# Front, retention, attention plan, MLP entry and the second MLP product's loads of a hybrid decoder block rearranged

## The chip, the cores and the metric

The kernel runs on one core of one Trainium2 chip. The metric is the device time of one execution in microseconds (us). A core has a matrix engine (TensorE, PE in the rows; its weight loads are PEld), VectorE (DVE), ScalarE (ACT), GpSimd (POOL) and SyncE (SP), which here only issues transfers (DMA).

## The reference, cut to what matters

One decoder block over 1024 tokens of width 1024, in fp32. Eight heads of causal differential attention and four heads of chunked retention run on one projection of the normed input; sigmoid gates merge them; then come a squared-ReLU MLP and a gate by a second embedding p.

```python
h = rms_norm(x, g_mix)
qa, ka, va, qr, kr, vr, gr, gate_a, gate_r = split(h @ w_in)
attn = softmax(c=0) - lam * softmax(c=1), causal ALiBi, then @ va      # 8 heads, 128 query rows at a time
ret  = chunkwise retention of qr, kr, vr (4 heads, chunks of 128), normed per head, times silu(gr)
mix  = sigmoid(gate_a) * (attn @ w_branch_diff) + sigmoid(gate_r) * (ret @ w_branch_ret)
x = x + mix @ w_out
x = x + square(relu(rms_norm(x, g_mlp) @ w_ff1)) @ w_ff2
x = x + gate(rms_norm(x, g_ple) @ w_ple_gate) * (p @ w_ple)
out = rms_norm(x, g_final)
```

## The kernel before

**Arithmetic.** Each fp32 operand is split into a high and a low part (`split`: a cast on ScalarE, L122, and a subtraction on VectorE, L123), and each product is three passes: high by high, high by low, low by high. The large products are Strassen-like: 2 x 2 blocks, with sums of blocks made on VectorE before they are split. A `product` (L303) and a `product_n` (L311) are 12 matmuls of 128x512; an `n_steps` (L200 to L202) or `t_steps` (L186 to L188) is 24 of them.

**Stages, in the order of the code.** (1) The front: rows of x are normed and turned (`norm_row`, L395), the products that make va and vr run (`va_first`, `v_first`, `v_rest`), and between them `fill` takes pieces of p @ w_ple from a queue (`pe_steps`, L443 and L454). A result bank of `v_first` is emptied by `v_spill`, a split on ScalarE and VectorE into the tile s2 ("s" in the rows). (2) 16 units of the in-projection, each with its block sums from `unit_prep`. (3) Retention, a head at a time: `ret_scores`, then `ret_chain` over eight chunks (L793), which ends in a norm (L801), then `ret_turn` (L810, evacuated at L813), with pieces of the gates' projection from the queue between (a queue step is six matmuls of 128x512). (4) Attention: 64 tiles of 128 queries, `scores` of the next tile (L860, its softmax on VectorE at L862 to L873, with exp on ScalarE), transposes of the last (`turn`, L887) and its product with v (`weigh`, L902), with gate pieces between. `PLAN` says how many queue steps a tile runs, `LAST` how many follow the 64th tile. (5) The branch products (`diff_half`), w_out in two sweeps over the eight row blocks of 128, half of the columns each; in the second sweep each block is normed (L1094, L1096), turned (L1104) and, from block 4 on, turned into five sums of blocks that the MLP wants (L1126 to L1132). (6) The first MLP product, 16 units (L303), the second (L1232), and the gate by p, whose product p @ w_ple is read back from `pe_d`.

Every engine runs its instructions in order, and that order is the order of the code, which the tile scheduler changes in places by the buffers. Tiles named S0 to S11, T0 to T7, Ga, Gb, s2, o, sq, raw, wh and wl are places in SBUF that one user after another takes. Banks of PSUM are named in

```python
BANKS = {"mm": 2, "qk": 3, "sm": 2, "po": 1}
```

so a third product that asks for "mm" waits until the first one's bank is emptied.

Of the kernel before, what the change touches and what calls it, by code (L numbers as in the profile page):

```python
# [36 lines left out]
PLAN = ((2, 2, 2, 2, 2, 2, 2, 2),) * HA  # L37
LAST = 16
# [24 lines left out]
def block_kernel(ctx: ExitStack, tc: tile.TileContext, t):  # L63
# [32 lines left out]
    pe_d = spill("pe_d", ST, D)  # L96
# [336 lines left out]
    def pe_steps():  # L433
        wph, wpl = [slot(s, F32R).rearrange("p (k n) -> p k n", k=2) for s in ("S10", "S11")]
        pT = [slot(s, F32R).rearrange("p (k s) -> p k s", k=2) for s in ("S6", "S9")]
        w = wp.rearrange("p (k n) -> p k n", k=2)
        for k in range(2):
            split(w[:, k, :], wph[:, k, :], wpl[:, k, :])
        for half in range(2):
            for k in range(2):  # L440
                pt = bank("sm")
                for j in range(4):
                    nc.tensor.transpose(out=pt[:, j * P:(j + 1) * P],  # L443
                                        in_=pn[:, half * 4 + j, k * P:(k + 1) * P], identity=ident)
                split(pt, pT[0][:, k, hs(half)], pT[1][:, k, hs(half)])
        yield
        for st in range(ST):
            ss_ = slice(st * P, (st + 1) * P)
            for n0 in (0, HALF):
                pe = bank("qk")  # L450
                mm = [(a[:, k, ss_], w[:, k, n0:n0 + HALF]) for k in range(2)
                      for a, w in ((pT[0], wph), (pT[0], wpl), (pT[1], wph))]
                for i, (l, r) in enumerate(mm):
                    nc.tensor.matmul(out=pe, lhsT=l, rhs=r, start=(i == 0), stop=(i == len(mm) - 1))  # L454
                o = slot("Ga", F32, (P, HALF), bufs=2)
                nc.scalar.copy(out=o, in_=pe)
# [893 lines left out]
```

## Time and profile before

| | us |
|---|---|
| median of three runs | 1982.68 (1981.89 to 1985.82) |
| the profiled execution | 1982.06 |
| its span, first to last instruction | 1980.3 |
| TensorE, 8976 matmuls, busy | 1906.2 |
| VectorE busy | 1307.5 |
| ScalarE busy | 875.9 |
| GpSimd busy | 96.4 |

Busy time of TensorE counts the overlap of pipelined matmuls, so a wait shows in the list of waits and in the idle time before a row, not in the share. The time of a run is the span and about 1.8 us around it.

### The profile page before, as it was taken

Reading aid. Unit: us, or ns where it says so; the run is one execution under the profiler, and the core shown is the slowest. Engines: PE = TensorE matmul, PEld = TensorE weight load, DVE = VectorE, ACT = ScalarE, POOL = GpSimd, SP = SyncE. Lnnn points to the kernel's source line nnn. Section 1 sums busy time; section 2 is a strip of 40 time slices with the busy share of each in tenths; the row PEclk is TensorE's granted clock in tenths of the full one; section 3 lists DMA queues with packets and bytes.
Section 4 is the critical chain, followed back from the end, with each engine's and each line's share of the span. In section 5 each row is a group of like instructions: output and inputs, shape, how many; then the busy total and the mean of one; then the engine's idle time right before and its main releaser. Section 6 shows DMA issues by size and latency. Waiting matters only on the chain.

```text
span 1980.3 us, 24252 instructions
## 1 busy us (share of the span) xinstructions
PE 1906.2 (96%) x8976; PEld 1569.8 (79%) x8976; DVE 1307.5 (66%) x2055; ACT 875.9 (44%) x1385; POOL 96.4 (5%) x112
## 2 busy tenths in 40 slices
PE   8999999999998999999998999799999999999998
PEld 6777788888887878787876887688888878888886
DVE  4777765543466578888886534877677676685754
ACT  6533444334444367666664313433333343333533
POOL 0200000000000011111110000000000000000000
PEclk9999999999999999999998999899999999999999
DMA  8644655532756775588624542254454896563513
GB/s 272 218 157 150 204 174 168 185 118 85 258 195 202 241 195 144 158 267 234 165 92 137 181 149 96 75 176 149 143 172 127 319 375 239 204 232 107 181 38 122
DMA packets 244342, 351.76 MB, mean 178 GB/s; under 512 B 16000, under 2 KB 127744, under 8 KB 242944
## 3 DMA queue, kind: packets, MB, share of 16 engines
q1 hardware_dynamic: 244224, 350.22, 54.9%
q8 instruction: 70, 1.15, 0.2%
q14 instruction: 48, 0.39, 0.1%
HBM read 239.54 MB, written 110.62 MB: 177 GB/s over the span
## 4 chain that ended last, share of the span: by engine, by line
PE 71%; DVE 12%; DMA 7%; ACT 4%; issue 3%; POOL 2%; SPq 1%; POOLq 0%; DVEq 0%; ACTq 0%
PE mm L303 17%; PE qk L303 13%; PE qk L1232 6%; PE mm L186 3%; PE mm L188 3%; PE mm L187 3%; PE mm L1232 3%; PE sm L1232 3%; PE mm L201 2%; PE qk L860 2%; PE mm L202 2%; PE mm L200 2%; PE po L1232 2%; PE mm L311 2%; DVE wl L123 2%
## 5 line engine op out<-in xcount | busy, mean ns | idle before, releaser
L186 PE MATMUL mm<-T,wh 128*128 128x512 f32 x384 | 152.6, 397 | 0.0
L188 PE MATMUL mm<-T,wl 128*128 128x512 f32 x384 | 152.0, 396 | 0.0
L187 PE MATMUL mm<-T,wh 128*128 128x512 f32 x384 | 152.0, 396 | 0.0
L867 ACT ACTIVATE S<-S,stat 128x256 f32<-128x256 f32 (+7 forms) x128 | 98.8, 774 | 36.3 <-DVE stat L862 34.6
L123 DVE TENSOR_TENSOR S<-T,S 128x1024 fp32r<-128x1024 f32 (+1 forms) x46 | 64.7, 1415 | 66.4 <-ACT S L122 66.4
L860 PE MATMUL qk<-S,S 128*128 128x512 f32 (+3 forms) x384 | 101.2, 363 | 2.4 <-DVE stat L862 1.9
L230 POOL TENSOR_TENSOR stat<-stat,mhalf 128x1 f32<-128x1 f32 (+1 forms) x28 | 24.4, 872 | 1437.3 <-DVE stat L228 1437.3
L303 PE MATMUL qk<-T,S 128*128 128x512 f32 x384 | 92.7, 390 | 0.0
L303 PE MATMUL mm<-T,raw 128*128 128x512 f32 x384 | 92.2, 389 | 0.0
L122 ACT CAST S<-T 128x1024 fp32r<-128x1024 f32 (+1 forms) x46 | 54.7, 1203 | 81.4 <-PE qk L303 54.7
L303 PE MATMUL mm<-wh,S 128*128 128x512 f32 x256 | 86.0, 397 | 4.3 <-ACT S L122 4.3
L303 PEld LDWEIGHTS qk<-T,S 128*128 128x128 f32 x384 | 72.4, 188 | 15.1
L303 PEld LDWEIGHTS mm<-T,raw 128*128 128x128 f32 x384 | 72.1, 188 | 15.0
L186 PEld LDWEIGHTS mm<-T,wh 128*128 128x128 f32 x384 | 72.5, 189 | 12.7 <-DVE Ga L991 0.4
L188 PEld LDWEIGHTS mm<-T,wl 128*128 128x128 f32 x384 | 72.3, 188 | 12.9
L187 PEld LDWEIGHTS mm<-T,wh 128*128 128x128 f32 x384 | 72.3, 188 | 12.4
L123 DVE TENSOR_TENSOR S<-sm,S 128x512 fp32r<-128x512 f32 (+2 forms) x116 | 64.4, 571 | 26.2 <-ACT S L122 25.5
L122 ACT CAST S<-S 128x512 fp32r<-128x512 f32 (+2 forms) x52 | 48.3, 950 | 60.7 <-PE qk L303 26.5
L862 DVE CUSTOM_DVE_ANT_0 S<-qk,Gb 128x512 f32<-128x512 f32 (+3 forms) x128 | 72.2, 582 | 3.7 <-ACT Gb L849 2.1
L860 PEld LDWEIGHTS qk<-S,S 128*128 128x128 f32 x384 | 61.4, 189 | 16.3 <-DVE stat L862 10.4
L122 ACT CAST S<-sm 128x512 fp32r<-128x512 f32 (+2 forms) x116 | 54.4, 496 | 44.6 <-PE sm L887 35.0
L122 ACT CAST wh<-S 128x1024 fp32r<-128x1024 f32 (+2 forms) x48 | 54.7, 1158 | 42.6 <-PE po L1232 19.6
(335 smaller groups left out, 4832.0 us busy)
## 6 DMA issues: line engine op xcount, KB each, us to landing
T<-in_w_ff SPq DMA_DIRECT2D x56, 512.0 KB, 5.7
S<-in_w_in SPq DMA_DIRECT2D x52, 512.0 KB, 5.0
S<-qk_d SPq DMA_DIRECT2D x96, 256.0 KB, 5.2
S<-in_w_ff SPq DMA_DIRECT2D x40, 512.0 KB, 6.2
qk_d<-T SPq DMA_DIRECT2D x32, 512.0 KB, 2.9
u_d<-S SPq DMA_DIRECT2D x16, 1024.0 KB, 5.2
u_d<-S SPq DMA_DIRECT2D x16, 768.0 KB, 7.0
T<-u_d SPq DMA_DIRECT2D x24, 512.0 KB, 4.5
```

The lines of the kernel that those rows point to most:

```text
L122: nc.scalar.copy(out=hi, in_=src)
L123: nc.vector.tensor_tensor(out=lo, in0=src, in1=hi.bitcast(F32), op=ALU.subtract)
L186: nc.tensor.matmul(out=ps, lhsT=wh(kt), rhs=ah, start=(kt == 0), stop=False)
L187: nc.tensor.matmul(out=ps, lhsT=wh(kt), rhs=al, start=False, stop=False)
L188: nc.tensor.matmul(out=ps, lhsT=wl(kt), rhs=ah, start=False, stop=(kt == KT - 1))
L200: nc.tensor.matmul(out=ps, lhsT=ah, rhs=wh(kt), start=(kt == 0), stop=False)
L201: nc.tensor.matmul(out=ps, lhsT=ah, rhs=wl(kt), start=False, stop=False)
L303: nc.tensor.matmul(out=ps, lhsT=x[:, k, :], rhs=y[:, k, :], start=(first and k == 0 and n == 0), stop=(k == 3 and n == 2), skip_group_chec ...
L860: nc.tensor.matmul(out=ps, lhsT=qs[:, c, qsl], rhs=kk[:, c, k0:k0 + kw], start=(m == 0), stop=(m == 1))
L862: nc.vector.tensor_tensor_reduce(out=pr[:, c, k0:k0 + kw], in0=ps, in1=bias[0][:, S - w + k0:S - w + k0 + kw], scale=-1.0, scalar=mx[:, 2 ...
L867: nc.scalar.activation(out=pc, in_=pc, func=AF.Exp, scale=-1.0, bias=mx[:, 2 * c + n:2 * c + n + 1], accum_out=z[:, c:c + 1])
L1232: nc.tensor.matmul(out=ps, lhsT=a[x][:, m, k, st * P:(st + 1) * P], rhs=b[y][:, m, k, :], start=(g == 0 and k == 0 and n == 0), stop=(g == ...
```

## The change

**Front.** `pe_steps` goes from here. In its place `early_gate` computes half of four gate row blocks (two weight groups, units 8 to 11 of the gates, first half of the tokens: 96 matmuls). The first products of va and vr take banks "qk", "qk", "qk", "po" in place of two "mm". p @ w_ple is now computed in the last stage, six matmuls ahead of each `n_steps`, and no longer written to memory and read back. `v_spill` for vr alternates between two tiles, and the tags of the first unit's block sums change.

**Retention.** A head's cos/sin input (`tmp`) is loaded a head earlier, `o` and `sq` alternate in `ret_turn`, and the queue holds 48 steps of gates for the four heads where it held 64, since the front has done 16.

**Attention.** `PLAN` moves steps to the end of a head, eight to the last tile; `LAST` is 10 for 16. The first `diff_half` weights are loaded early, and `reload(ya_d, ya, 1)` comes after the last tile.

**w_out and the MLP entry.** The two sweeps become one: `row_half(st, n)` makes half a row block, `row_norm` norms it, `row_turn` turns it, and a later block's `row_half` stands between a norm and its turn. The two subtractions of L1130 and L1132 move from VectorE to GpSimd, and the splits for s3 and s4 from one per block to one of all four, after the last block. The first product pairs of units 0 and 1 (`unit_begin`, L303) are issued around the last two turns.

**The second MLP product.** The eight loads of x1 (512 KB each) move from its beginning to after the fourth group of its second sum.

```diff
-PLAN = ((2, 2, 2, 2, 2, 2, 2, 2),) * HA
-LAST = 16
+PLAN = ((2, 2, 2, 2, 2, 2, 1, 3),) * (HA - 1) + ((2, 2, 2, 2, 2, 2, 2, 8),)
+LAST = 10
...
+    def early_gate(g, raw_tag, tags):
...
+        for u in range(2):
+            yield from t_steps([[a11, a12]], 0, lambda kt: w[0][:, kt, u * P:(u + 1) * P],
+                               lambda kt: w[1][:, kt, u * P:(u + 1) * P],
+                               lambda ps: gate_out(2 * g + u, 0, AF.Sigmoid, ps))
...
-            g = slot("s2", F32R, (P, 1024)).rearrange("p (a n) -> p a n", a=2)
+            g = slot(("s2", "Gb")[st % 2 if d is vr_d else 0], F32R, (P, 1024)).rearrange("p (a n) -> p a n", a=2)
...
-    queue.append(pe_steps())
+    early = [early_gate(4, "T6", ("S6", "S9")), early_gate(5, "T7", ("S10", "S11"))]
...
     def va_first(i):
-        pb[i] = bank()
+        pb[i] = bank(("qk", "qk", "qk", "po")[i])
         v_first(pb[i], p1a, i, w11)
...
+    ps = [bank(("qk", "qk", "qk", "po")[i]) for i in range(4)]
+    va = v_prep(C_VA)
+    v_first(ps[0], p1r, 0, w11)
+    v_first(ps[1], p1r, 1, w11)
     second_half(5)
...
     def in_prep(n):
-        return unit_prep(w_in, *units[n][0:2], ("S1", "S0")[n % 2], "S3", ("S2", "wh", "wl"))
+        return unit_prep(w_in, *units[n][0:2], ("S1", "S0")[n % 2], "S2", ("wh", "wl", "wh"))
...
-        tmp = slot("S2").rearrange("p (a s) -> p a s", a=2)
+        tmp = slot(("S2", "S6")[h % 2]).rearrange("p (a s) -> p a s", a=2)
...
-                f = slot("o", F32, (P, HALF))
+                f = slot(("o", "sq")[half], F32, (P, HALF))
...
+    for g in (4, 5, 6, 7):
+        queue.append(gate_steps(g, AF.Sigmoid, (1,) if g < 6 else (0, 1)))
...
+            if c:
+                fill(between)
...
     att_tile(HA * ST, LAST)
+    reload(ya_d, ya, 1)
...
+    def row_half(st, n):
+        if st not in rows:
+            rows[st] = raw_tile()
+            nc.sync.dma_start(out=rows[st], in_=x_d[st * P:(st + 1) * P, :])
+        ps = bank("qk")
+        run(n_steps(mixed, st, lambda kt: wq[n][kt // 4][0][:, kt % 4, :],
+                    lambda kt: wq[n][kt // 4][1][:, kt % 4, :], ps))
+        add(rows[st][:, hs(n)], ps, rows[st][:, hs(n)])
...
-        nc.vector.tensor_tensor(out=f11[:, :, cs], in0=f11[:, :, cs], in1=f21, op=ALU.subtract)
-        put(f11[:, :, cs], s3)
-        nc.vector.tensor_tensor(out=f12[:, :, cs], in0=f12[:, :, cs], in1=f2, op=ALU.subtract)
-        put(f12[:, :, cs], s4)
+        add(f11[:, :, cs], f11[:, :, cs], f21, ALU.subtract, nc.gpsimd)
+        add(f12[:, :, cs], f12[:, :, cs], f1, ALU.subtract, nc.gpsimd)
...
+    row_half(7, 1)
+    row_turn(6)
+    row_norm(7)
+    unit_begin(0)
+    row_turn(7)
+    s3, s4 = op_tiles("S0", "S6"), op_tiles("S7", "S8")
+    for f, (hi, lo) in ((f11, s3), (f12, s4)):
+        prep_step(0)
+        for k in (0, 2):
+            split(f[:, k:k + 2, :], hi[:, k:k + 2, :], lo[:, k:k + 2, :])
+    prep_step(0)
+    unit_begin(1)
...
+            if us == (2, 4) and g == 3:
+                for st in range(ST):
+                    nc.sync.dma_start(out=xs(st), in_=x1_d[:, st, :])
...
+            pe = bank("qk")
+            mm = [(a[:, k, ss_], w[:, k, n0:n0 + HALF]) for k in range(2)
+                  for a, w in ((pT[0], wph), (pT[0], wpl), (pT[1], wph))]
```

TensorE in the front of the kernel before, between the first products for vr of row groups 2 and 3 (L311 is `product_n`, L454 is p @ w_ple; a name is the result's bank and number, then the two operands):

```order
L311 MATMUL mm_753<-wh_535,T_10_110 128x512
L454 MATMUL qk_781<-S_36_219,S_38_221 128x512
L454 MATMUL qk_781<-S_37_220,S_38_221 128x512
L454 MATMUL qk_781<-S_36_219,S_39_222 128x512
L311 MATMUL mm_754<-wh_535,T_9_109 128x512
L311 MATMUL mm_754<-wl_536,T_9_109 128x512
```

The same two products in the change (L310 is now `product_n`):

```order
L310 MATMUL qk_505<-wh_383,T_7_104 128x512
L310 MATMUL qk_505<-wl_384,T_7_104 128x512
L310 MATMUL qk_505<-wh_383,T_8_105 128x512
L310 MATMUL po_506<-wh_383,T_7_104 128x512
L310 MATMUL po_506<-wl_384,T_7_104 128x512
L310 MATMUL po_506<-wh_383,T_8_105 128x512
```

The pieces of p @ w_ple between them are gone, and the four products have four banks of their own where they had two in turn.

TensorE at the last attention tile before: the end of `weigh` for tiles 60 and 61 (L902), the transposes of tiles 62 and 63 (L887; S_1503 is tile 62's probabilities, S_1514 tile 63's), and the first branch pieces (L186, L187):

```order
L902 MATMUL po_9010<-S_1496_8908,S_1356_8264 128x128
L902 MATMUL po_9010<-S_1497_8909,S_1356_8264 128x128
L902 MATMUL po_9010<-S_1496_8908,S_1356_8264 128x128
L887 MATMUL sm_9044<-ident,S_1503_8934 128x128 x4
L887 MATMUL sm_9051<-ident,S_1503_8934 128x128 x3
L887 MATMUL sm_9093<-ident,S_1514_8987 128x128 x4
L887 MATMUL sm_9100<-ident,S_1514_8987 128x128 x4
L186 MATMUL mm_9156<-S_1466_8783,wh_9138 128x512
L187 MATMUL mm_9156<-S_1467_8784,wh_9138 128x512
L902 MATMUL po_9010<-S_1522_9042,S_1356_8264 128x256
```

In the change (L895 is `weigh`, L880 the transposes, S_1463 tile 62's and S_1474 tile 63's), the first rows after `weigh`, and in the second fence the rows around tile 63's transposes, which come 22 rows behind tile 62's:

```order
L895 MATMUL po_8836<-S_1456_8727,S_1312_8073 128x128
L880 MATMUL sm_8863<-ident,S_1463_8753 128x128 x4
L880 MATMUL sm_8870<-ident,S_1463_8753 128x128 x3
L187 MATMUL mm_8905<-S_1424_8594,wl_8613 128x512
L185 MATMUL mm_8934<-S_1422_8592,wh_8612 128x512
```

```order
L185 MATMUL mm_8934<-S_1424_8594,wh_8612 128x512
L186 MATMUL mm_8934<-S_1425_8595,wh_8612 128x512
L187 MATMUL mm_8934<-S_1424_8594,wl_8613 128x512
L880 MATMUL sm_8947<-ident,S_1474_8806 128x128 x4
L880 MATMUL sm_8954<-ident,S_1474_8806 128x128 x4
L185 MATMUL mm_8934<-S_1424_8594,wh_8612 128x512
```

Twenty-two matmuls of a branch product now stand between the two tiles' transposes, where there was none.

TensorE at the MLP entry before, at the transposes of row block 7 (L1104), between the first products of unit 0 (L303, bank 10534) and of unit 1 (bank 10663); the next rows after unit 1's first twelve are unit 0's third product, on the sum S_1741:

```order
L303 MATMUL qk_10534<-S_1649_10018,T_1740_10515 128x512
L303 MATMUL qk_10534<-S_1648_10017,T_1740_10515 128x512
L1104 MATMUL sm_10483<-ident,Gb_10475 128x128 x4
L1104 MATMUL sm_10488<-ident,Gb_10475 128x128 x4
L303 MATMUL mm_10663<-S_1646_10015,T_1754_10570 128x512
...
L303 MATMUL mm_10663<-S_1646_10015,T_1754_10570 128x512
L303 MATMUL mm_10533<-wh_10289,S_1741_10520 128x512
```

In the change (L1116 transposes row block 7, L201 ends a `row_half`, L302 is `product`):

```order
L201 MATMUL qk_10182<-S_1535_9253,T_1518_9106 128x512
L1116 MATMUL sm_10208<-ident,Gb_10167 128x128 x4
L1116 MATMUL sm_10213<-ident,Gb_10167 128x128 x4
L302 MATMUL mm_10241<-S_1580_9577,wh_10114 128x512
...
L302 MATMUL qk_10242<-S_1582_9579,wh_10114 128x512
L1116 MATMUL sm_10271<-ident,Gb_10232 128x128 x4
L1116 MATMUL sm_10276<-ident,Gb_10232 128x128 x4
L302 MATMUL mm_10320<-S_1580_9577,wh_10179 128x512
...
L302 MATMUL qk_10321<-S_1582_9579,wh_10179 128x512
L302 MATMUL qk_10351<-T_1626_9929,T_1686_10300 128x512
```

Block 7's transposes now follow 24 matmuls of unit 0, and 24 of unit 1 stand between them and the first product that reads their sums (s1, T_1626), where twelve stood.

VectorE at the same place before, up to the norm row of block 7 (L1096; L1090 adds w_out's result to the residual row, L1126 and L1127 make the sums, L123 the low parts):

```order
L1126 TENSOR_TENSOR sq_10428<-sm_10422,o_10427 128x512
L228 TENSOR_SCALAR stat_10478<-stat_10476 128x1
L123 TENSOR_TENSOR T_1740_10515<-T_1738_10511,T_1740_10515 128x1024
L1127 TENSOR_TENSOR Ga_10429<-sq_10428,S_1650_10019 128x512
L123 TENSOR_TENSOR T_1695_10288<-sq_10428,T_1694_10287 128x4x128
L1130 TENSOR_TENSOR S_1650_10019<-S_1650_10019,o_10427 128x4x128
L123 TENSOR_TENSOR wl_10290<-Ga_10429,wh_10289 128x4x128
L1132 TENSOR_TENSOR S_1651_10020<-S_1651_10020,Ga_10429 128x4x128
L123 TENSOR_TENSOR wl_10292<-S_1650_10019,wh_10291 128x4x128
L1096 SCALAR_TENSOR_TENSOR Gb_10475<-raw_10445,stat_10480,s_1645_10013 128x1024
```

In the change, up to the norm row of block 7 (L1106; L314 is any sum or difference, L122 the low parts, L279 the weights' sums, the add into raw_10024 the second half of row block 7, for which it waits for TensorE):

```order
L122 TENSOR_TENSOR T_1627_9930<-sq_10154,T_1626_9929 128x4x128
L122 TENSOR_TENSOR T_1625_9928<-sm_10148,T_1624_9927 128x4x128
L314 TENSOR_TENSOR sq_10154<-sq_10154,S_1584_9581 128x512
L279 TENSOR_TENSOR T_1651_10113<-wl_10110 128x512
L279 TENSOR_TENSOR T_1651_10113<-wl_10110,T_1651_10113 128x512
L122 TENSOR_TENSOR S_1629_9932<-sq_10154,S_1628_9931 128x4x128
L314 TENSOR_TENSOR raw_10024<-qk_10182,raw_10024 128x512
L122 TENSOR_TENSOR T_1686_10300<-T_1651_10113,T_1686_10300 128x1024
L314 TENSOR_TENSOR sq_10219<-sm_10213,o_10218 128x512
L227 TENSOR_SCALAR stat_10235<-stat_10233 128x1
L279 TENSOR_TENSOR wl_10110<-wl_10110 128x512
L1106 SCALAR_TENSOR_TENSOR Gb_10232<-raw_10024,stat_10237,s_1579_9575 128x1024
```

The two differences of L1130 and L1132 and their low parts have left the stretch; weights' sums and the add of block 7's last half have entered it.

## Rows read from the trace of the kernel before

**Rows 1.** The page's first line.

```profile
span 1980.3 us, 24252 instructions
```

**Rows 2.** By stage: stretch, length, busy time of the five engines, TensorE clock, DMA, GB/s.

```profile
690.00:1040.00 350.00, 338.62 (x1844) 277.65 (x1844) 293.78 (x707) 241.01 (x470) 51.03 (x61) 1.00 0.65 181
...
1250.00:1276.00 26.00, 18.14 (x57) 13.13 (x58) 23.46 (x37) 12.79 (x21) 1.40 (x1) 0.74 0.21 57
1276.00:1563.00 287.00, 287.00 (x1267) 237.75 (x1266) 205.59 (x286) 105.02 (x138) 0.00 (x0) 1.00 0.51 165
```

**Rows 3.** TensorE's waits in the front: engine, line, releaser; us, times, longest.

```profile
PE mm L311 <- DVE s L123: 7.4, 3, 3.8
...
PE mm L311 <- DVE Gb L315: 1.8, 1, 1.8
PE mm L303 <- ACT wh L122: 1.5, 1, 1.5
```

**Rows 4.** TensorE behind two of these waits: start, length, instruction, idle before.

```profile
84.69 0.59 PE L311 MATMUL mm<-wh,T 128*128 128x512 f32 x1 [3.83 <-DVE s L123]
...
221.07 4.14 PE L303 MATMUL mm<-S,wh 128*128 128x512 f32 x10 [0.53 <-DVE wh L123]
```

**Rows 5.** TensorE's waits in retention.

```profile
PE sm L810 <- DVE S L801: 4.2, 3, 1.4
PE qk L793 <- DVE S L123: 2.1, 4, 1.5
...
PE sm L730 <- DVE o L813: 1.0, 1, 1.0
```

**Rows 6.** TensorE's waits in attention.

```profile
PE sm L887 <- DVE S L873: 5.8, 11, 0.9
```

**Rows 7.** TensorE at the last attention tile.

```profile
1043.70 3.57 PE L902 MATMUL po<-S,S 128*128 128x256 f32 x17 [1.99 <-DVE S L123]
...
1054.62 1.94 PE L887 MATMUL sm<-ident,S 128*128 128x128 f32 x8 [6.40 <-DVE S L873]
...
1058.51 2.85 PE L902 MATMUL po<-S,S 128*128 128x256 f32 x23
```

**Rows 8.** TensorE's waits, w_out and MLP entry.

```profile
PE mm L303 <- ACT S L122: 4.3, 1, 4.3
...
PE mm L303 <- DVE T L123: 3.2, 2, 2.7
PE mm L303 <- ACT T L122: 1.7, 2, 1.4
```

**Rows 9.** TensorE at the MLP entry.

```profile
1247.22 1.06 PE L1104 MATMUL sm<-ident,Gb 128*128 128x128 f32 x8 [0.54 <-DVE Gb L1096]
...
1253.80 4.64 PE L303 MATMUL mm<-S,T 128*128 128x512 f32 x10 [2.71 <-DVE T L123]
...
1263.57 2.56 PE L303 MATMUL mm<-S,T 128*128 128x512 f32 x10 [0.52 <-DVE T L123]
```

**Rows 10.** VectorE at the MLP entry.

```profile
1257.28 1.28 DVE L1096 SCALAR_TENSOR_TENSOR Gb<-raw,stat,s 128x1024 f32<-128x1024 f32 x1
...
1266.44 0.68 DVE L1130 TENSOR_TENSOR S<-S,o 128x512 f32<-128x512 f32 x1
1267.04 0.68 DVE L123 TENSOR_TENSOR wl<-Ga,wh 128x512 fp32r<-128x512 f32 x1
```

**Rows 11.** VectorE in the front, 58 to 63 us.

```profile
58.21 2.31 DVE L123 TENSOR_TENSOR wl<-S,wh 128x1024 fp32r<-128x1024 f32 x1 [0.21 <-ACT wh L122]
...
62.14 1.21 DVE L123 TENSOR_TENSOR wl<-S,wh 128x1024 fp32r<-128x1024 f32 x1
```

**Rows 12.** GpSimd in the same stretch.

```profile
58.14 1.30 POOL L315 TENSOR_TENSOR T<-T,o 128x512 f32<-128x512 f32 x1 [8.95 <-DVE sq L315]
59.39 2.27 POOL L315 TENSOR_TENSOR T<-T,sq 128x512 f32<-128x512 f32 x1
```

**Rows 13.** TensorE's waits from the second MLP product on.

```profile
PE mm L1232 <- ACT T L122: 1.5, 1, 1.5
```

More of the change, by code (lines that the diff above doesn't have):

```diff
@@ L547, in block_kernel @@
     w11 = split_b(b11)
-    queue.append(pe_steps())
+    early = [early_gate(4, "T6", ("S6", "S9")), early_gate(5, "T7", ("S10", "S11"))]
+    for g in early:
+        next(g)
+        queue.append(g)
     p1a = wide("S2")
@@ L599, in block_kernel @@
     vr = v_prep(C_VR)
-    v_rest(va_d, p1a, va, lambda: next(vr))
+    v_rest(va_d, p1a, va, lambda: next(vr), ready)
     def att_put(h):
@@ L678, in block_kernel, with cols_steps @@
     hT = [[a11, a12], [a21, a22]]
-    def cols_steps(act, w, c0, evac):
+    def cols_steps(act, w, c0, evac, halves=(0, 1)):
         wh, wl = load_cols(w, c0)
-        for half in range(2):
+        for half in halves:
             for u in range(2):
@@ L1027, in diff_half @@
     def diff_half(g, half):
-        if half == 0:
+        if half == 0 and g not in held:
             held[g] = load_cols(t["w_branch_diff"][0], g * 256)
-        if not mixed:
-            mixed.extend(act_tiles(T_TAGS))
+        if (g, half) == (0, 0):
+            mixed.extend(act_tiles(T_TAGS[0:4], 1))
+            load_early()
+        if (g, half) == (0, 1):
+            mixed.extend(act_tiles(T_TAGS[4:8], 1))
         wh, wl = held[g]
@@ new lines, in block_kernel, with row_norm @@
+    f11, f12 = wide("S9"), wide("S10")
+    rows, xns = {}, {}
+    def row_half(st, n):
[6 more added lines that the diff above has]
+        add(rows[st][:, hs(n)], ps, rows[st][:, hs(n)])
+    def row_norm(st):
+        row = rows.pop(st)
+        nc.sync.dma_start(out=x1_d[:, st, :], in_=row)
+        xns[st] = slot("Gb", F32, (P, 1024))
@@ L1136, in block_kernel @@
+    row_half(0, 1)
+    row_half(0, 0)
+    for st in range(4):
+        row_norm(st)
+        row_half(st + 1, 0)
+        row_turn(st)
+        if st < 3:
+            row_half(st + 1, 1)
+    a22, s1, s2o = op_tiles("T0", "T1"), op_tiles("T2", "T3"), op_tiles("S11", "S3")
+    row_half(5, 0)
+    row_half(6, 0)
+    row_half(4, 1)
+    row_norm(4)
+    row_half(7, 0)
+    row_turn(4)
+    row_half(5, 1)
+    row_norm(5)
     UNITS = DFF // 256
     w1, w2 = t["w_ff1"][0], t["w_ff2"][0]
+    preps, opsof, begun = {}, {}, {}
@@ new lines, in prep_step, with unit_begin @@
+    def prep_step(u):
+        if u >= UNITS:
+            return
+        if u not in preps:
+            preps[u] = unit_prep(w1, u * P, DFF // 2 + u * P, "wl", "T4", ("wh", "T5", "T6"))
+        opsof[u] = next(preps[u])
+    def unit_begin(u):
+        ops = opsof[u]
+        ux = slot(("T7", "S9")[u % 2]).rearrange("p (i s) -> p i s", i=4)
+        pa, pb = bank(), bank("qk")
+        p1 = slot("Ga", F32, (P, HALF), bufs=2)
+        product(pa, ops["b11"], a11, True)
+        nc.scalar.copy(out=p1, in_=pa)
+        product(pb, ops["b21"], a12, True)
+        add(ux[:, 2, :], pb, p1)
+        relu2(ux[:, 2, :])
+        begun[u] = pa, ux
@@ L1160, in block_kernel @@
         u2 = slot(("o", "sq")[u % 2], F32, (P, HALF))
         p5 = slot(("s2", "Gb")[u % 2], F32, (P, 1024))[:, 0:HALF]
-        product(pa, now["b11"], a11, True)
-        nc.scalar.copy(out=p1, in_=pa)
-        product(pb, now["b21"], a12, True)
-        add(ux[:, 2, :], pb, p1)
-        relu2(ux[:, 2, :])
-        ops = next(nxt, None)
+        if u:
+            prep_step(u + 1)
         product(pa, now["t2"], s2o, False)
```

274 lines of the change are left out of this document (126 added, 148 removed).

## The prediction

> **What bounds the kernel now.** I read the stage table first, then TensorE's waits stage by stage, then the timelines around the largest. TensorE is the engine that the end follows: in the first MLP product it runs 1267 matmuls in 287.00 us without a gap [rows 2], 0.2265 us each, and I use that as the price of one matmul of 512 columns. Matmul count and sizes are the same before and after (8976), so the change can only take away idle time, add some, or change the clock. The waits are the whole sum, and they lie in four places. In the front the products wait for a bank that `v_spill` has not emptied: three times, 7.4 us [rows 3]. In retention the turn of a head waits for its norm, three times 1.4 [rows 5]. At the last attention tile TensorE waits 6.40 for the softmax of a tile with nothing else to issue [rows 7]. At the MLP entry three sorts of wait come to 9.2 [rows 8], and there the granted clock over 26 us is 0.74 [rows 2]. The idle time costs twice: behind a long wait TensorE runs at its lower level. Ten matmuls behind the 2.71 us wait took 4.64, ten behind a short one 2.56 [rows 9], so 2.1 us more; ten behind the waits at the in-projection's entry took 4.14 [rows 4], 1.6 more.
>
> **Front.** The products for va and vr get four banks, so the third no longer needs the first one's bank at once, and the 7.4 goes. The 1.8 for Gb goes with the block sums being made earlier (`ready`), the 1.5 and 0.53 at the entry [rows 3, 4] with the first unit's tags, which no longer wait for tiles that the last `v_rest` still reads. That is 11.2. The clock's fall behind the 3.83 us wait (a matmul of 0.59 behind it) and at the entry [rows 4] is priced at 1.6 each: 14.4 in all. The gate pieces that come in (96 matmuls, 21.7 us) replace the 96 of p @ w_ple, which move to the last stage, where they are on the path; retention loses the same 96. These three cancel, if retention becomes shorter by what it loses. Bounds: if one bank wait stays at its longest, 3.8, with its clock, 9.0; nothing more than the 14.4 is listed.
>
> **Retention.** Alternating `o` and `sq` frees the tile that the next evacuation wants, 1.0, and the order of the pieces at the turn covers the norm: 4.2 [rows 5]. I take both, 5.2; what waits in the chunk chain (L793, 2.1) stays. Below, nothing goes, since a head then has 12 queue steps for 16 to lay over the same work; above, 7.3.
>
> **Attention.** 64 tiles with the same VectorE work, which is busy 293.78 of 350 us [rows 2]; steps move from one tile to another. The waits at the transposes are 5.8 [rows 6]. I take no change, with that 5.8 as the bound to either side.
>
> **Last tile.** Eight queue steps, 48 matmuls, 10.9 us, now stand around tile 63's softmax, more than the 6.40 that was missing; the wait of 1.99 for `weigh` goes with the steps moved ahead of it. Behind these two waits 17 matmuls took 3.57 where 23 of the same took 2.85, 1.46 too much, and eight transposes 1.94 where eight took 1.06 [rows 7, 9], 0.88 too much. Sum 10.7. Moving the reload of the second half of ya behind the tile adds a load ahead of the next branch product; ten gate and branch steps (60 matmuls, 13.6 us) cover it, and if they did not, part of this gain would be the price.
>
> **w_out and MLP entry.** Between a norm and its turn stand 24 matmuls, 5.4 us, as before, so I leave the 0.54 a block [rows 9] where it is. The three waits of 9.2 [rows 8] go, with two falls of the clock at 2.1: 13.4. But VectorE's work stays near the path. From the norm row of block 6 to that of block 7 it has nine instructions at 0.60 from start to start, one of twice the size at 1.2 and one norm row at 1.28 [rows 10]: 8.0 us, in which TensorE has eight transposes (0.9) and 24 matmuls, 6.3. That leaves 1.7. From block 7's norm row to s1 it is about 6.8 against 6.3, another 0.5, and to s2o 0.3 more than a product of 12. The two subtractions that go to GpSimd are saved (1.2 a block), but not free: while GpSimd did the same two, the low part on VectorE took 2.31 where it takes 1.21 [rows 11, 12], 1.1 for each GpSimd instruction that meets it. Between zero and 2.2 a block I take 1.1 for the one block that is in the tight stretch. With one fall of the clock, 2.1, that gives back 5.7. Net 7.7; bounds 2 (the give-back twice) and 17.7 (nothing stays, and eight times 0.54 goes too).
>
> The Trainium skill has a rule on this, in SBUF — State Buffer, section "SBUF: two separate sides": GpSimd and a VectorE instruction with two SBUF inputs share a port pair under an exclusive lock, and whoever comes second is blocked for the whole of the other. By that rule every GpSimd subtraction of 1.30 would hold VectorE for up to 1.30, and the give-back would be 7.2 with both instructions of the block met (2.6 for 1.1), the net 6.2. The front's trace agrees in kind: 1.1 was lost beside a 1.30.
>
> **Second MLP product.** The eight residual loads leave the head of SyncE's queue, and the operands' transfers land earlier: 1.5 [rows 13]. Where they go, after the fourth group of the second sum, half of the product is still ahead of their reader; if it weren't, they would cost the same 1.5.
>
> **Sum.** 14.4 + 5.2 + 0 + 10.7 + 7.7 + 1.5 = 39.5 from the profiled execution's 1982.06: 1942.6, in span 1980.3 [rows 1] to 1940.8. The median of the runs is 0.6 above the profiled one, so 1943. A change under 0.2%, 4 us, can't be told from none here.
>
> **Rivals.**
> More goes than I count (chance 0.18): the 5.7 at the MLP entry and the 5.8 of attention, the eight 0.54 of w_out and the 2.1 of the chunk chain go too: 17.9 less, 1925. For it speaks that each is small and that every stage gets some rearrangement; against it that VectorE's share in attention is what it was.
> VectorE holds (0.17): in retention and at the MLP entry the wait only moves, the 5.2 and the 7.7 are not seen and the attention's waits double (5.8): 1943 + 18.7 = 1962. For it speaks that VectorE is busy 23.46 of 26 us at the MLP entry [rows 2]. It would end as waits for DVE at the transposes of the last three blocks.
> GpSimd locks VectorE out in the last two blocks, both instructions each (0.08): 5.2 in place of 1.1, 1947. The rule named above makes this one; rows 11 and 12 bear it out once.
> The gates' cover is missed (0.04): this one ends slower. Retention keeps 48 steps of 64; if the chain over the chunks (32 of them) now waits at L793 as long as its longest wait, 1.5 [rows 5], in each, that is 48 us, and the kernel takes 1991. It decides from 39.5 / 32 = 1.23 us a chunk. Against it: one step a chunk is set apart from the number held in the queue and does not change; the steps lost are those behind the turn.
> The change does not do what it says (0.03): the banks are not what the front waits for, and the last tile waits for another operand; then the rest stays within 4 us of 1982.
> The forecast keeps 0.50.
>
> **How the numbers follow.** Forecast, more, VectorE and GpSimd together hold 0.93 and are all faster by over 4 us; no change 0.03, slower 0.04. The forecast's own bounds are 14.4 to 9.0 in the front, 7.3 to 0 in retention, 5.8 either way in attention, and 17.7 to 2 at the MLP entry; added as independent they give some 11 to either side, 1932 to 1954. The range that leaves out less than 2 in 10 takes in the ends of the two large rivals: 1922 to 1962.
>
> **What would show it.** The changed profile should have no wait of L311's successor for the spill tile in the front, a last tile without a gap over 1 us, retention shorter by about 27 us (21.7 moved and 5.2), the last stage longer by about 22, and a w_out and MLP entry with waits of 6 to 10 us left, all for VectorE. Waits at the chunk chain or at the transposes in attention that come to more than 15 us, or a retention that is not 20 us shorter, would make the prediction wrong.

## The result and the profile after

The changed kernel takes 1955.84 us (median of 4 runs, 1954.34 to 1957.98), the kernel before 1982.29 in the same series: ratio 0.9866, 95% interval 0.9848 to 0.9885. It is faster by 26.5 us; 39.5 were forecast.

The first rows are the span and four stages (stretch, its length, busy time of PE, PEld, DVE, ACT and POOL, granted clock, DMA share, GB/s); below them, from the list of TensorE's waits over the whole run, the largest.

```profile
span 1954.1 us, 24125 instructions
```

```profile
511.00:644.00 133.00, 123.41 (x724) 105.15 (x722) 94.87 (x198) 63.28 (x154) 7.40 (x4) 0.97 0.75 244
644.00:1033.00 389.00, 373.64 (x2013) 306.36 (x2013) 321.95 (x753) 262.64 (x502) 53.81 (x64) 0.99 0.65 183
...
1109.00:1246.00 137.00, 128.04 (x578) 104.51 (x577) 77.29 (x99) 44.86 (x71) 18.37 (x16) 0.98 0.26 86
...
1834.00:1954.00 120.00, 111.62 (x508) 92.12 (x507) 48.66 (x88) 35.19 (x70) 5.51 (x10) 0.98 0.10 36
```

```profile
PE sm L880 <- DVE S L866: 7.6, 15, 0.9
PE sm L1116 <- DVE Gb L1106: 6.2, 2, 3.9
PE qk L784 <- ACT Gb L121: 4.3, 2, 3.4
PE qk L853 <- DVE stat L855: 3.9, 9, 1.7
PE mm L302 <- DVE s L314: 2.9, 1, 2.9
...
PE sm L802 <- DVE S L792: 2.1, 2, 1.4
PE mm L302 <- DVE S L122: 1.9, 1, 1.9
```

The waits for a spill [rows 3] are gone, and the 6.40 us at the last tile [rows 7]. In their place stand three that are new, or longer than before: the retention chain's products (L784) wait for ScalarE's cast into Gb, the transposes of two row blocks at the MLP entry (L1116) wait up to 3.9 us for their norm (0.6 at most before), and a unit of the in-projection waits 2.9.

To see where the 26 us come from, I took each stage's length from its first matmul to the next stage's first (the front's from the start of the span) and subtracted its matmuls at the spacing they have without a wait (0.2267 us for 512 columns, 0.175 for 384, 0.118 for 256, 0.109 for a transpose and 0.061 for another of 128). What is left is idle time and slow clock:

| stage | matmul time before, after | left over before | after | gain | forecast |
|---|---|---|---|---|---|
| front | 185.4, 183.7 | 27.3 | 16.5 | 10.8 | |
| in-projection | 310.1, 307.4 | 4.2 | 3.3 | 0.9 | 14.4 with the front |
| retention | 128.6, 109.1 | 24.7 | 24.2 | 0.5 | 5.2 |
| attention and last tile | 331.4, 343.3 | 49.4 | 45.9 | 3.5 | 0 and 10.7 |
| w_out, MLP entry | 122.6, 122.6 | 22.3 | 13.9 | 8.4 | 7.7 |
| second MLP product | 308.2, 311.3 | 2.6 | 0.8 | 1.8 | 1.5 |
| branch, first MLP product, last stage | 452.7, 461.8 | 1.8 | 1.3 | 0.5 | 0 |

The expectations below give the front as 27.5 and 16.3, each 0.2 us from the value here; no reading rests on that difference.

Each figure comes from one profile. The profiles of the kernels below that leave a stage of the changed kernel as it is show how far it varies by itself: front 15.2 to 16.6 us, in-projection 3.3 to 5.3, retention 20.8 to 26.2, attention with the last tile 42.9 to 45.9, w_out and MLP entry 12.1 to 14.6, second MLP product 0.7 to 1.5. One more profile of the old code of retention and of the second MLP product has 22.7 and 0.6 where this table has 24.7 and 2.6. So the gains of front, last tile and MLP entry are clear of this spread, and those of the in-projection, of retention and of the second MLP product are not.

The 21.7 us of matmuls that move did cancel: retention has 19.5 us less of them, the last stage 20.4 more, at no idle time. Front and w_out with the MLP entry came out near the forecast. What is missing is retention, and 7.2 us in attention.

At the last tile the two sets of transposes (tile 62, tile 63) now have no wait ahead of them; start, length and instruction on TensorE:

```profile
1021.36 0.95 PE L880 MATMUL sm<-ident,S 128*128 128x128 f32 x7
...
1027.21 1.04 PE L880 MATMUL sm<-ident,S 128*128 128x128 f32 x8
```

Taken head by head in the same way, head 7 with the last tile goes from 16.9 us left over to 5.3, so 11.6 came where 10.7 were forecast. Head 4 goes from 6.1 to 11.5 and head 0 from 4.0 to 6.5, and that takes most of it back. In the other profiles with this code head 4 has 10.5 to 12.2 and head 0 4.6 to 6.1, so head 4's loss is the sure one.

### The profile page after: what moved, and what is told of

Read it like the earlier page. It is cut to its first block, busy times and chain, and to the rows that moved or that the text cites. A ratio compares the mean times of both kernels' runs of the same rounds, so it can differ in the third digit from the quotient of the medians.

```text
span 1954.1 us, 24125 instructions
## 1 busy us (share of the span) xinstructions
PE 1898.3 (97%) x8976; PEld 1568.2 (80%) x8976; DVE 1316.5 (67%) x2047; ACT 873.2 (45%) x1370; POOL 108.5 (6%) x120
## 4 chain that ended last, share of the span: by engine, by line
PE 76%; DVE 10%; DMA 6%; issue 4%; ACT 3%; POOL 2%; SPq 0%; POOLq 0%; DVEq 0%; ACTq 0%
PE mm L302 17%; PE qk L302 13%; PE qk L1279 6%; PE mm L187 4%; PE mm L185 4%; PE mm L186 4%; PE sm L1279 3%; PE mm L1279 3%; PE qk L853 2%; PE po L1279 2%; PE po L895 2%; PE qk L310 2%; DMA S<-in_w_in 2%; PE mm L199 1%; PE mm L200 1%
## 5 line engine op out<-in xcount | busy, mean ns | idle before, releaser
L185 PE MATMUL mm<-T,wh 128*128 128x512 f32 x352 | 140.2, 399 | 0.0
L186 PE MATMUL mm<-T,wh 128*128 128x512 f32 x352 | 139.9, 397 | 0.0
L187 PE MATMUL mm<-T,wl 128*128 128x512 f32 x352 | 139.3, 396 | 0.0
L121 ACT CAST wh<-S 128x1024 fp32r<-128x1024 f32 (+1 forms) x60 | 69.2, 1167 | 94.0 <-issue 33.6
L229 POOL TENSOR_TENSOR stat<-stat,mhalf 128x1 f32<-128x1 f32 (+1 forms) x28 | 22.7, 809 | 1352.2 <-DVE stat L227 1352.2
L302 PE MATMUL mm<-S,T 128*128 128x512 f32 x384 | 94.3, 395 | 2.6 <-DVE S L122 1.9
L302 PE MATMUL mm<-T,raw 128*128 128x512 f32 x384 | 92.4, 389 | 2.9 <-DVE s L314 2.9
L302 PE MATMUL mm<-S,wh 128*128 128x512 f32 x384 | 93.1, 391 | 0.0
L302 PE MATMUL qk<-S,wh 128*128 128x512 f32 x384 | 92.2, 389 | 0.0
L302 PEld LDWEIGHTS mm<-S,T 128*128 128x128 f32 x384 | 73.0, 191 | 19.1 <-DVE S L122 2.3
L302 PEld LDWEIGHTS mm<-T,raw 128*128 128x128 f32 x384 | 72.0, 188 | 18.3 <-DVE s L314 3.3
L122 DVE TENSOR_TENSOR T<-T,T 128x1024 fp32r<-128x1024 f32 (+2 forms) x28 | 40.3, 1449 | 66.2 <-ACT T L121 66.2
L302 PEld LDWEIGHTS mm<-S,wh 128*128 128x128 f32 x384 | 72.5, 189 | 15.0
L302 PEld LDWEIGHTS qk<-S,wh 128*128 128x128 f32 x384 | 72.1, 188 | 15.0
L121 ACT CAST S<-sm 128x512 fp32r<-128x512 f32 (+2 forms) x116 | 54.5, 493 | 49.4 <-PE sm L880 30.6
L853 PEld LDWEIGHTS qk<-S,S 128*128 128x128 f32 x384 | 62.6, 192 | 16.9 <-DVE stat L855 11.5
L187 PEld LDWEIGHTS mm<-T,wl 128*128 128x128 f32 x352 | 66.6, 189 | 11.7
L185 PEld LDWEIGHTS mm<-T,wh 128*128 128x128 f32 x352 | 66.7, 190 | 11.2
L186 PEld LDWEIGHTS mm<-T,wh 128*128 128x128 f32 x352 | 66.5, 189 | 11.0
```

The source lines that it names most:

```text
L121: nc.scalar.copy(out=hi, in_=src)
L122: nc.vector.tensor_tensor(out=lo, in0=src, in1=hi.bitcast(F32), op=ALU.subtract)
L185: nc.tensor.matmul(out=ps, lhsT=wh(kt), rhs=ah, start=(kt == 0), stop=False)
L186: nc.tensor.matmul(out=ps, lhsT=wh(kt), rhs=al, start=False, stop=False)
L187: nc.tensor.matmul(out=ps, lhsT=wl(kt), rhs=ah, start=False, stop=(kt == KT - 1))
L302: nc.tensor.matmul(out=ps, lhsT=x[:, k, :], rhs=y[:, k, :], start=(first and k == 0 and n == 0), stop=(k == 3 and n == 2), skip_group_chec ...
```

## The experiments

**The high parts of the turn out of Gb, 1941.0 us.** In the changed kernel `ret_turn` writes its high parts to Gb, from which they are stored to `yr_d`; before, they went to sq. That edit is part of the change, and the text ahead of the prediction does not list it:

```diff
-                hi = slot("sq", F32R, (P, HALF))
...
+            his = slot("Gb", F32R, (P, 1024)).rearrange("p (a s) -> p a s", a=2)
```

The next head's chain also keeps its state in Gb, and the bias table with which attention begins lies there too. ScalarE at a head's border, and VectorE's first score row in attention:

```profile
560.57 0.71 ACT L121 CAST Gb<-S 128x256 fp32r<-128x256 f32 x2 [3.60 <-DMA yr_d<-Gb]
```

```profile
662.92 0.29 DVE L855 CUSTOM_DVE_ANT_0 S<-qk,Gb 128x128 f32<-128x128 f32 x1 [7.72 <-DMA Gb<-in_alibi]
```

Each waits for a transfer: 3.60 us for the store out of Gb, and 7.72 for the load of the bias into Gb, the same tile. SyncE issues that load right behind the last store out of Gb; in the run below, in which the turn leaves Gb alone, it does so 13 us earlier, 8 of them counted from attention's first matmul (first two rows the changed kernel, third row that run):

```profile
654.50 0.32 SPq L88 DMA_DIRECT2D yr_d<-Gb  x1
...
656.78 0.33 SPq L838 DMA_DIRECT2D Gb<-in_alibi  x1
```

```profile
643.90 0.41 SPq L839 DMA_DIRECT2D Gb<-in_alibi  x1
```

```diff
+        vh = slot(("S4", "S10")[h % 2], F32R).rearrange("p (e a s) -> p e a s", e=2, a=2)
...
-            his = slot("Gb", F32R, (P, 1024)).rearrange("p (a s) -> p a s", a=2)
+            his = vh[:, e]
```

> The changed kernel, with the high parts of a retention turn kept where the finished head's v lay (S4 or S10), no longer in Gb. If the expected gain of retention was lost to a new wait, because the next head's chain and the first attention tile want Gb while its stores to memory are still under way, then TensorE's waits for ScalarE's cast into Gb (4.3 us, longest 3.4) and VectorE's wait of 7.7 us for the bias table go, idle time of TensorE in retention falls from about 24 us to about 18, and the kernel takes 1948 to 1952 us. If retention is held by VectorE's work in a head, the waits only move to another row: 1955 to 1957 us.

Measured: 1941.02 us (ratio 0.9803, 0.9788 to 0.9817), 14.8 less than the changed kernel by the medians, 12.5 by the ratios, 14.7 by the spans (1954.1 and 1939.4), and better than both figures expected. Retention's rest falls from 24.2 to 19.2, attention's from 45.9 to 37.7. Attention's fall is far outside the spread given above, retention's by little: the lowest of the other kernels with this code has 20.8, and a second kernel with this edit (below) 20.4. TensorE's waits in retention are now

```profile
PE qk L784 <- ACT Gb L121: 2.0, 1, 2.0
PE sm L766 <- DVE S L751: 1.9, 1, 1.9
PE sm L803 <- DVE S L792: 0.7, 1, 0.7
```

and VectorE's wait for the bias is gone. The one wait of 2.0 for a cast into Gb that is left lies in the first head and is of another kind: that cast stands behind one on ScalarE that waits 2.42 us for gate weights:

```profile
524.79 1.04 ACT L121 CAST wh<-raw 128x1024 fp32r<-128x1024 f32 x1 [2.42 <-DMA raw<-in_w_in]
```


**Out of Gb for the last head alone, 1947.5 us.**

```diff
+        if h == HR - 1:
+            vh = slot("S10", F32R).rearrange("p (e a s) -> p e a s", e=2, a=2)
...
-            his = slot("Gb", F32R, (P, 1024)).rearrange("p (a s) -> p a s", a=2)
+            his = vh[:, e] if h == HR - 1 else slot("Gb", F32R, (P, 1024)).rearrange("p (a s) -> p a s", a=2)
```

> The changed kernel with the high parts of a retention turn out of Gb for the last head alone. It parts the two losses that go with Gb. If the late bias table at attention's entry is what drew gate steps into head 0 (136 matmuls, 114 with all heads out of Gb) and left head 4 short (72 and 101), then here head 0 has about 114, head 4 about 100, idle time in attention falls from 45.9 to about 38 us, retention keeps its 24 us, and the kernel takes 1946 to 1949 us. If head 4 is short for another reason, attention stays above 44 us and the kernel at 1954 to 1956.

Measured: 1947.53 us (0.9825, 0.980 to 0.985). Gate and branch matmuls of 512 columns by head, and what is left over:

| | head 0 | head 4 | attention | retention |
|---|---|---|---|---|
| changed kernel | 136, 6.5 us | 72, 11.5 us | 45.9 us | 24.2 us |
| last head out of Gb | 93, 5.6 | 92, 6.9 | 39.5 | 24.5 |
| all heads out of Gb | 114, 4.7 | 101, 5.0 | 37.7 | 19.2 |

So the two losses part: with the last head alone out of Gb, the wait for the bias and most of attention's loss are gone, and retention stays where it was. The way from the late bias to head 4 is not shown. Head 4's rest goes with its count of pieces (72, 92 and 101, and 81 with 6.1 us in the kernel before), which fits pieces being spent in head 0 and missing in head 4. But head 0 has 93 here, where about 114 was expected, the figure with all heads out of Gb, and the scheduler's reasons are not in a trace.

**The plan undone, 1955.1 and 1955.4 us.** First two steps a tile and none between the halves of a tile's scores, with eight and ten at the last tile:

```diff
-PLAN = ((2, 2, 2, 2, 2, 2, 1, 3),) * (HA - 1) + ((2, 2, 2, 2, 2, 2, 2, 8),)
+PLAN = ((2, 2, 2, 2, 2, 2, 2, 2),) * (HA - 1) + ((2, 2, 2, 2, 2, 2, 2, 8),)
...
-            m = int(n > 1 and (b + 1) % ST > 3)
+            m = 0
```

> The changed kernel with two queue steps after each of the first 63 attention tiles, as before, none between the two halves of a tile's scores, and still eight and then ten steps at the last tile. If the new shape of the plan is what costs some 8 us in heads 0 and 4 (idle time of TensorE beyond the matmuls 11.5 us in head 4, 6.5 in head 0, where before 6.1 and 4.0), the idle time in these heads falls back to some 4 to 6 each, and the kernel takes 1948 to 1951 us; but the last tile of heads must then show the waits of before, up to 1.1 each. If the loss comes from what is ahead of attention and from the order of the queue, not from the plan, head 4 keeps over 10 us and the time stays at 1954 to 1957 us.

Measured: 1955.06 (0.9873, 0.9855 to 0.9891); head 4 keeps 11.2 us. The first expectation falls: the plan is not what costs attention its 7 us. Then also two steps at the last tile and 16 behind it:

```diff
-PLAN = ((2, 2, 2, 2, 2, 2, 1, 3),) * (HA - 1) + ((2, 2, 2, 2, 2, 2, 2, 8),)
-LAST = 10
+PLAN = ((2, 2, 2, 2, 2, 2, 2, 2),) * HA
+LAST = 16
...
-            m = int(n > 1 and (b + 1) % ST > 3)
+            m = 0
```

> The changed kernel with the plan of before, two steps after every tile and 16 behind the last, none between the halves of a tile's scores. The cover at the last tile is taken away: if it is worth what the forecast gave it (10.7 us), the wait of about 6 us for the last softmax and the fall of the clock behind it are back, and the kernel takes some 10 to 12 us more than the one that differs from it in the last tile alone (two steps a tile, then eight and ten): 1959 to 1963 us if that one takes 1949 to 1951. If the wait is covered by the later reload or by the early loads of the change, under 4 us more.

Measured: 1955.41 (0.9875, 0.986 to 0.9891), head 7 at 5.6 us. The eight steps, on which the forecast rested this term, are not needed for it.

**Plan, early weights and reload undone together, 1967.1 us.** To the last diff come

```diff
-                held[0] = load_cols(t["w_branch_diff"][0], 0)
...
+                reload(ya_d, ya, 1)
             att_tile(h * ST + i, PLAN[h][i])
     att_tile(HA * ST, LAST)
-    reload(ya_d, ya, 1)
```

> The changed kernel with three edits around the last attention tile undone together: the plan of before (two steps a tile, 16 behind the last), the first branch weights loaded only when their product asks for them, and the reload of the second half of ya ahead of the last tile. The plan alone undone cost nothing. In TensorE's written order one branch matmul now stands between the transposes of the last two tiles, as before, where any one or two of the three undone leave 22 or more. If the order is what took the 6.4 us wait away, the wait and the fall of the clock are back: idle time of head 7 some 16 to 17 us in place of 5.3, the kernel 1965 to 1969 us. If the last softmax is earlier for another reason, it stays within 3 us of 1956.

Measured: 1967.09 (0.993, 0.9902 to 0.9957), head 7 at 19.2 us. The wait is back, by another name: TensorE's waits around the last tile here, and below them ScalarE in the kernel before at the same place.

```profile
PE mm L185 <- ACT wh L121: 6.1, 1, 6.1
PE po L895 <- DVE S L122: 2.2, 1, 2.2
```

```profile
1054.52 1.05 ACT L122 CAST wh<-raw 128x1024 fp32r<-128x1024 f32 x1 [3.92 <-DMA raw<-in_w_branch_diff]
```

In the kernel before the weights of the first branch pieces landed at 1054.5, just when the softmax was ready too. TensorE had nothing to issue in the gap: on SyncE's queue these weights come behind the last part of the reload.

```profile
1047.06 0.32 SPq L975 DMA_DIRECT2D raw<-ya_d  x1
1050.96 4.52 SPq L135 DMA_DIRECT2D raw<-in_w_branch_diff  x3
```

With early weights and late reload in place the gap stays closed under the new plan and under the old (1955.8 and 1955.4 us). Whether one of these two is enough alone, or the new plan without them, was not run.

**The subtractions of the MLP entry back on VectorE, 1948.7 us.**

```diff
-        add(f11[:, :, cs], f11[:, :, cs], f21, ALU.subtract, nc.gpsimd)
-        add(f12[:, :, cs], f12[:, :, cs], f1, ALU.subtract, nc.gpsimd)
+        add(f11[:, :, cs], f11[:, :, cs], f21, ALU.subtract)
+        add(f12[:, :, cs], f12[:, :, cs], f1, ALU.subtract)
```

> The changed kernel with the two subtractions of the row blocks 4 to 7 on VectorE in place of GpSimd. VectorE gets 8 instructions of 0.60 us from start to start, 4.8 us, and loses the holding up that shows as 1.66 to 1.99 us for instructions of 0.68 and 1.22 (about 2.2 us a block, 8.8 in all). If GpSimd's lock on VectorE is what keeps the waits at the MLP entry (3.9, 2.4, 1.9 us), they shrink by 1 to 2 us each and the kernel takes 1951 to 1954 us. If VectorE's queue there is long by its own work, the 4.8 us come on top of the waits: 1956 to 1960 us.

Measured: 1948.69 (0.9837, 0.9819 to 0.9856), 7.1 less than the changed kernel (6.2 by the spans, 5.7 by the ratios); w_out and the MLP entry fall from 13.9 to 8.4 us left over. First VectorE and GpSimd in the changed kernel, beside the subtractions of block 5 (the last VectorE row is beside one of block 6, the first beside none), then TensorE's waits there in both, the changed kernel's first:

```profile
1204.22 0.69 DVE L122 TENSOR_TENSOR T<-sq,T 128x512 fp32r<-128x512 f32 x1
...
1206.74 1.66 DVE L279 TENSOR_TENSOR T<-wl,T 128x512 f32<-128x512 f32 x1
1208.32 1.78 DVE L122 TENSOR_TENSOR S<-sq,S 128x512 fp32r<-128x512 f32 x1
...
1217.14 1.99 DVE L122 TENSOR_TENSOR T<-wl,T 128x1024 fp32r<-128x1024 f32 x1
```

```profile
1206.25 1.60 POOL L314 TENSOR_TENSOR S<-S,o 128x512 f32<-128x512 f32 x1 [3.26 <-DVE sq L314]
1207.81 1.74 POOL L314 TENSOR_TENSOR S<-S,sq 128x512 f32<-128x512 f32 x1
```

```profile
PE sm L1116 <- DVE Gb L1106: 6.2, 2, 3.9
PE mm L302 <- DVE S L122: 1.9, 1, 1.9
```

```profile
PE sm L1116 <- DVE Gb L1106: 2.6, 1, 2.6
PE qk L302 <- DVE S L122: 1.1, 1, 1.1
PE qk L302 <- ACT S L121: 1.0, 1, 1.0
PE sm L1116 <- ACT S L121: 0.8, 1, 0.8
```

The sum of 0.68 takes 1.66, the low part of 0.68 takes 1.78, the split of 1.22 takes 1.99, each beside a GpSimd subtraction. The ends alternate: GpSimd's first ends at 1207.85, VectorE's sum 0.55 later at 1208.40, GpSimd's second at 1209.55, VectorE's low part 0.55 later at 1210.10. That is what the rule would give that the forecast weighed (the Trainium skill, SBUF — State Buffer, "SBUF: two separate sides"): each waits for the whole of the other's instruction. The two edits together were run too.

> The changed kernel with both edits that were faster than it: the high parts of a retention turn in the old place of v, and the two subtractions at the MLP entry on VectorE. The two losses lie in different stages, so if each is what its own run showed, 1941.0 against 1955.8 us and 1948.7 against 1955.8, they add to 14.8 + 7.1: 1932 to 1936 us. If part of what the first gave back came by a shift that the second undoes, or the other way, it stays at 1938 to 1941.

Measured: 1935.54 (0.9775, 0.9756 to 0.9794). 14.8 and 7.1 off 1955.8 make 1933.9; the measured median lies 1.6 above it, inside what was expected. The two gains add. It is the fastest version here, 20.3 us under the changed kernel and 45 under the kernel before of its series (1980.56).

**The loads of x1 first, 1967.8 us.**

```diff
+    for st in range(ST):
+        nc.sync.dma_start(out=xs(st), in_=x1_d[:, st, :])
...
-            if us == (2, 4) and g == 3:
-                for st in range(ST):
-                    nc.sync.dma_start(out=xs(st), in_=x1_d[:, st, :])
```

> The changed kernel with the eight loads of x1 at the beginning of the second MLP product, as before. If they delay its first operands, the wait of 1.5 us and some of 0.4 on the operand splits are back in the second group: idle time of that stage 2.5 us in place of 0.8, the kernel 1957 to 1958 us. If the new places of the first operands' buffers are what removed it, nothing changes.

Measured: 1967.78 in one run, 13.9 us left over in this stage for 0.8. The wait, and SyncE's queue in this kernel and then in the changed one:

```profile
1541.84 1.22 PE L1281 MATMUL mm<-wh,wh 128*128 128x512 f32 x2 [9.78 <-ACT wh L121]
```

```profile
1515.77 3.21 SPq L1244 DMA_DIRECT2D S<-x_d  x5
...
1526.45 3.02 SPq L1244 DMA_DIRECT2D S<-x_d  x3
1529.52 1.06 SPq L1251 DMA_DIRECT2D S<-in_w_ff  x2
```

```profile
1512.71 1.02 SPq L1249 DMA_DIRECT2D S<-in_w_ff  x2
...
1533.57 6.21 SPq L1305 DMA_DIRECT2D S<-x_d  x8
```

The second group's weights are issued 17 us later, behind all eight loads. So in the changed kernel the place of the loads is worth 13.1 us of this stage. It is not shown that the move gained anything over the kernel before: there the loads stand first too, and the profile of that kernel with the spill tile alternating (below), whose second MLP product is the same code, has 0.6 us left over, and on TensorE only this wait:

```profile
PE mm L1232 <- DVE T L123: 0.2, 1, 0.2
```

The 1.5 us of [rows 13], on which the forecast rested this term, is not in every run. Why the same place costs 13 us in the changed kernel was not taken apart.

**Banks and spill tiles in the front.** Two banks in turn for the first products, which also asks for another order of the products for vr:

```diff
-        pb[i] = bank(("qk", "qk", "qk", "po")[i])
+        pb[i] = bank()
...
-    ps = [bank(("qk", "qk", "qk", "po")[i]) for i in range(4)]
+    ps = [bank(), bank()]
...
+    for i in (0, 1):
+        v_first(ps[i], p1r, i, w21, vr_d)
+    fill(1)
+    ps += [bank(), bank()]
```

> The changed kernel with the first products for va and vr in two banks by turns (and the early gates in a bank of their own), so that the third product of vr again needs a bank that a spill has to empty. If the banks are what the front waited for, waits of TensorE on the spill's split of some 3 to 4 us in the longest are back before the third and fourth product, with a fall of the clock behind them: idle time of the front 20 to 23 us in place of 16.3, the kernel 1959 to 1963 us. If the rest of the front's new order covers the spill, the front stays at 16 to 17 us.

Measured: 1955.61 in one run, front 18.2 us left over for 16.5; no wait for the spill. Then two banks with the one tile s2 for all spills:

```diff
-            g = slot(("s2", "Gb")[st % 2 if d is vr_d else 0], F32R, (P, 1024)).rearrange("p (a n) -> p a n", a=2)
+            g = slot("s2", F32R, (P, 1024)).rearrange("p (a n) -> p a n", a=2)
```

> The changed kernel with two banks for the first products and with the one spill tile s2. Two banks alone left the front at 18.1 us of idle time (16.3 with four). If the single spill tile is what holds the banks, the waits on the spill's split are back here, 3 us or more in the longest: 21 to 24 us of idle time in the front. If neither is the cause, it stays at 18.

Measured: 1954.34 in one run, front 19.9; the spill's wait is back once with 1.5 us. With four banks and one tile:

> The changed kernel with every spill of va and vr through the one tile s2, as before, and its four banks. In the kernel before, ScalarE's cast into s2 waited 2.15 us for the store of the spill ahead of it (at 82.69), and the bank was released only behind that. If the one tile and the two banks are each enough alone to bring the wait, the front's idle time goes from 16.3 to 20 us or more; if four banks cover it, the front stays at 16 to 18 us.

This run tells nothing: TensorE was slowed in all of it (matmuls of 512 columns 0.47 us apart at a granted clock of 1.00 between 400 and 1600 us, a granted clock of 0.56 from 1800 us on), and it took 3462 us. Last, the alternating spill tile alone in the kernel before:

```diff
-            g = slot("s2", F32R, (P, 1024)).rearrange("p (a n) -> p a n", a=2)
+            g = slot(("s2", "Gb")[st % 2 if d is vr_d else 0], F32R, (P, 1024)).rearrange("p (a n) -> p a n", a=2)
```

> The kernel before with one line of the change: the spills of vr alternate between s2 and Gb. Nothing else. If the single tile caused the front's waits for a spill (7.4 us of three waits, 3.8 and 3.0 the longest, with a fall of the clock behind one), most of it goes with this line: idle time of the front from 27.5 to 20 to 23 us and the kernel 4 to 7 us faster than before. If the two banks are the cause, under 2 us.

Measured: 1978.99 (0.999, 0.9976 to 1.0005), front 26.9 us left over for 27.3: under the 4 to 7 us that the single tile would have had to give. TensorE's waits there:

```profile
PE qk L311 <- ACT wh L122: 3.3, 1, 3.3
...
PE mm L311 <- DVE s L123: 2.0, 1, 2.0
...
PE qk L311 <- DVE wl L123: 1.0, 1, 1.0
```

The waits for the spill go from 7.4 to 2.0 us, and 4.3 us of new ones for the next products' operands (wh, wl) take their place.

## Why the prediction was right, and where it was off

The time lies in the range and in the way that was forecast; the forecast's own figure was 13 us too low. It also lies 2 us above the forecast's own bounds (1932 to 1954): the range holds it because it was stretched to the end of a rival, "VectorE holds", that gave another reason than the one found. Of the signs named, most came: no wait for the spill tile, a last tile without a gap, waits of 8.1 us at the MLP entry for VectorE. Retention became 20.0 us shorter (153.3 to 133.3) where 27 were named, just at the limit of 20 that would have spoken against the prediction.

**Front, 14.4 forecast with the in-projection, 11.7 measured.** The size is near by luck, for the reason given is not borne out. "The products for va and vr get four banks, so the third no longer needs the first one's bank at once, and the 7.4 goes": two banks cost 1.7 us, two banks and one spill tile 3.4, with no more time for the kernel in one run of each. In the kernel before, freeing the spill tile alone gave under 1 us in the front, since new waits for the next products' operands (4.3 us) took most of what it saved. What gives the other 7 us no run here takes apart: the order of loads, operands and products is new as well, and the cause stays open. In the in-projection a new wait of 2.9 us, 20 us behind its start, stands for the 2.0 removed at its entry.

**Retention, 5.2 forecast, 0.5 measured.** The step that failed is "alternating `o` and `sq` frees the tile that the next evacuation wants": that it does, L730's wait is gone, but the high parts went into Gb, and the forecast did not follow who wants Gb next. Of the norm's 4.2, which the order of the pieces was to cover, 2.1 stayed. With the high parts elsewhere the stage has 19.2 and 20.4 in two profiles, where the old code has 24.7 and 22.7, so a gain of some 4.

**Attention, 0 forecast, 8 lost** (5 to 8 over the profiles with this code). "64 tiles with the same VectorE work" was true and missed the point: the loss comes from the same use of Gb by the last head's turn, which makes the bias late; how that reaches head 4 is argued, not shown. All of it is back, to 37.7, when Gb is left alone; before, with the last tile's 11.6 taken off, it was 37.8.

**Last tile, 10.7 forecast, 11.6 measured.** Right in size. But "eight queue steps, 48 matmuls, 10.9 us, now stand around tile 63's softmax" is not the cause by itself: with the old plan the gain stays, and it goes only with early weights and the late reload undone as well. The forecast saw in the later reload only a possible price.

**w_out and MLP entry, 7.7 forecast, 8.4 measured,** near by luck, from the wrong rows. "I leave the 0.54 a block where it is" failed: there are no waits at the first four turns, since each block's last sum no longer stands behind the splits of the block ahead in VectorE's queue (that order is read from the two traces, not tried apart). The three waits of 9.2, which were to go, came back as 3.9, 2.4 and 1.9 on the turns of blocks 5 and 7 and the last split. GpSimd's part, taken at 1.1 for one block, measured 5.5 left over in the stage and 5.7 to 7.1 in the time: the rival "GpSimd locks VectorE out" had the mechanism, its 5.2 was near, and it got 0.08.

**Second MLP product, 1.5 forecast, 1.8 measured.** The agreement shows nothing: the same old code had 0.6 left over in another profile, less than the changed kernel's 0.8. What is shown is that the old place would have cost 13 us in the changed kernel.

Of the rivals, "VectorE holds" named 1962 and the waits at the MLP entry, but its place in retention and attention was a buffer, not VectorE. That the chunk chain would wait 1.5 us in each of 32 chunks did not happen (4.5 us in all at L784).

## What to carry to other kernels

When an edit gives a value a new buffer, follow that buffer to its next users: here one 512 KB tile with a store under way held the next head's first cast, then the next stage's first table, and cost 12 to 15 us, most of it in the next stage, far from the edited line. A subtraction moved to an idle engine is not free if that engine and the busy one hold each other up, so read the length of the busy engine's instructions beside it. And when several edits each cover a gap, undoing one may show nothing; undo them together before calling any the cause. Last, take a wait of 1 or 2 us for a gain only when a second profile of the same code has it too.

## What was not expected of the hardware

Instructions of VectorE and GpSimd that meet take turns, instruction by instruction: VectorE's 0.68 became 1.66 to 1.78 beside GpSimd subtractions of 1.60 and 1.74. And one run of the changed kernel's variant with s2 alone had TensorE at about half speed from its start, at first with a granted clock of 1.00, while the busy times of VectorE (1332 us) and ScalarE (875) were near those of the changed kernel (1317 and 873). It is one run, and its cause stays open.
